# Raw weight chunks through three buffers, then five, then seven

## The chip, the cores and the metric

The kernel runs on one core of a Trainium2 chip. The metric is the device time of one execution in microseconds (us). Five engines work side by side, each through its own queue in order: TensorE (PE in the profile; its weight loads are PEld), VectorE (DVE), ScalarE (ACT), GpSimd (POOL) and SyncE (SP). SP computes nothing here and issues most of the DMAs; POOL issues most of the others.

## The reference, cut to what matters

A two-layer generator works on 256 context tokens and 256 latent tokens, 1024 wide, in fp32. Layer 0 mixes tokens with a bidirectional mLSTM, layer 1 with latent attention (MLA) over context and latent tokens. A gated convolutional FFN (2816 wide) follows each mixer. Around each sub-layer stands a modulation by a condition vector and a post-layer normalisation:

```python
ml = _modulation(c, ada_w[i], ada_b[i])
hl = _modulate(x, ml[0], ml[1])
...
x = _layer_norm(ALPHA * x + ml[2] * yl, ln_g[i, 0], ln_b[i, 0])
f = _conv_ffn(_modulate(x, ml[3], ml[4]), ffn_w_in[i], ffn_conv_w[i], ffn_conv_b[i], ffn_w_out[i])
x = _layer_norm(ALPHA * x + ml[5] * f, ln_g[i, 1], ln_b[i, 1])
```

The context stream needs layer 0 whole, and of layer 1 only its keys and values. The output is the latent stream.

## The kernel before

**Products.** Each fp32 operand is split in two: a high part, rounded to the matmul's type, and a low part, the rest. A product then takes three matmuls (`mm3`, lines 311 to 315): high by high, high by low, low by high.

**Weights.** All weights but the modulations' lie in the array `ws` as chunks of 128 x 1024 fp32 (512 KB; a few are narrower), in the order in which they are used. `_plan` writes that order down: up, og, v, gates, qk, mout (mLSTM), fin0, fout0 (first FFN, with the three dkv chunks of attention ahead of the last six of fout0), ukn, uv, dq, uqr, uqn, aout (attention), fin1, fout1 (second FFN). `Stream` takes each chunk through three steps. `_load` (line 236) lets SP issue a DMA into a raw buffer (tag "raw", three of them). `_split` (line 244) casts the high part on ScalarE (line 257) and subtracts it on VectorE for the low part (line 258); from then on the raw buffer is free. After that `_split` loads further, until three chunks (`NRAW`) beyond the split ones are on their way. `use` hands the parts to the matmuls.

**Two kinds of split buffers.** A narrow chunk goes into one of three pairs (tag "w", the profile's tile w). A wide one, marked in `_plan`, takes two of the 31 general tiles (tag "u", tile wu), so that the last chunks of a stage and the first of the next can be ready at once: `TAIL` says how many chunks at a stage's end are multiplied row tile by row tile, `WIDE` how many are split into general tiles. The general tiles also hold activations, probabilities and normalised rows. `pump` and `st.limit` say how far splits may go at a boundary.

**Boundaries.** After mout, fout0, aout and fout1 stands a normalisation (`ln_rows`, lines 943 to 987): VectorE multiplies by the gate (953), adds the residual (954), takes statistics (956, 958); ScalarE takes the root (960), VectorE the reciprocal (961) and the negative mean (963), and both write the normalised rows (984, 985, 982). `ln_T` (1003) transposes them on TensorE (1011), applies the modulation (1018, 1020) and splits the result (1023, 1024). The context's dkv rows go through `rms` (1140 to 1143) and `dkv_T` (1191).

**Other users of the tags.** Modulations after the start are made on VectorE in the background: `ada_bg` (line 428) loads 128 x 1024 blocks of `ada_w` into two tiles of tag "ar" and sums into two tiles of tag "acc". The order on SP shows the last of these done during fin0. `rope_load` (line 1238) puts the rotary table into the two "ar" tiles; its last reader is `rope_rows`, for the queries, before attention's heads. The start-up also uses both tags, once.

**Order.** The order of instructions on each engine outside the start-up is set by a scheduler that goes by priorities and by when it takes operands and buffers to be ready. So a buffer that is free earlier can also change the order of other work in the queues of PE, DVE, ACT and SP.

Of the kernel before, what the change touches and what calls it, by code (L numbers as in the profile page):

```python
# [7 lines left out]
F32 = mybir.dt.float32  # L8
# [21 lines left out]
CW = 1024  # L30

NB, NRAW, NU = 3, 3, 31
# [189 lines left out]
class Stream:  # L222


    def __init__(self, k, ids, order, ws):
# [4 lines left out]
        self.limit = self.n  # L230
        self.raw, self.hl = {}, {}

    def skip(self, n):
        self.nl = self.ns = self.nu = n

    def _load(self):
        k, j = self.k, self.nl
        n, cols = self.ids[self.order[j][0]]
        t = k.pool.tile([128, CW], F32, tag="raw", name="raw", bufs=NRAW)
        k.nc.sync.dma_start(t[:, :cols], self.ws[n, :, :cols])  # L240
        self.raw[j] = t
        self.nl += 1

    def _split(self):
        k, j = self.k, self.ns
        key, wide = self.order[j]
        cols = self.ids[key][1]
        while self.nl <= j:
            self._load()
        raw = self.raw.pop(j)  # L250
        if wide:
            h, l = [k.pool.tile([128, CW], F32R, tag="u", name="wu", bufs=NU) for _ in range(2)]
        else:
            w = k.pool.tile([128, 2, CW], F32R, tag="w", name="w", bufs=NB)
            h, l = w[:, 0], w[:, 1]
            self.live.append(j)
        k.nc.scalar.copy(h[:, :cols], raw[:, :cols])  # L257
        k.nc.vector.tensor_sub(l[:, :cols], raw[:, :cols], h[:, :cols])  # L258
        self.hl[j] = (h, l)
        self.ns += 1  # L260
        while self.nl < min(self.ns + NRAW, self.n):
            self._load()

    def use(self, key, hold=False):
# [1326 lines left out]
```

## Time and profile before

| | us |
|---|---|
| median of three runs (lowest, highest) | 1431.02 (1429.1, 1434.94) |
| the profiled execution | 1429.89 |
| its span, first to last instruction | 1428.1 |
| TensorE busy | 1398.6 |
| VectorE busy | 980.5 |
| ScalarE busy | 642.3 |
| mean granted TensorE clock (share of full) | 0.996 |

The page's groups give the price of one instruction: a cast of a chunk on ScalarE (L257) 1.05 us, a subtraction on VectorE (L258) 1.21 us, a raw load 3.9 us from issue to landing (median of 300). Matmuls are pipelined: one of 512 columns is listed with 0.39 us, but the timeline shows them 0.23 us apart. A line "A <- B: total, times, longest" among the waits says how long engine A stood idle until B released it. In the timeline the columns are start, duration, engine, line, operation, tiles and count, with the idle time before it and its releaser in brackets. In the stretches, the columns are the length, then busy time and count by engine, the clock, the DMA engines' busy share and GB/s.

### The profile page before, as it was taken

Reading aid. Unit: us, or ns where it says so; the run is one execution under the profiler, and the core shown is the slowest. Engines: PE = TensorE matmul, PEld = TensorE weight load, DVE = VectorE, ACT = ScalarE, POOL = GpSimd, SP = SyncE. Lnnn points to the kernel's source line nnn. Section 1 sums busy time; section 2 is a strip of 40 time slices with the busy share of each in tenths; the row PEclk is TensorE's granted clock in tenths of the full one; section 3 lists DMA queues with packets and bytes.
Section 4 is the critical chain, followed back from the end, with each engine's and each line's share of the span. In section 5 each row is a group of like instructions: output and inputs, shape, how many; then the busy total and the mean of one; then the engine's idle time right before and its main releaser. Section 6 shows DMA issues by size and latency. Waiting matters only on the chain.

```text
span 1428.1 us, 18819 instructions
## 1 busy us (share of the span) xinstructions
PE 1398.6 (98%) x7095; PEld 1176.5 (82%) x7095; DVE 980.5 (69%) x1437; ACT 642.3 (45%) x972; POOL 100.1 (7%) x185
## 2 busy tenths in 40 slices
PE   7999999999999999999999999999999999899997
PEld 3788888888888888888888888888887998899986
DVE  6696778885775666666787444444567888777755
ACT  6554231224334254464553333334364665555542
POOL 0010110003001010210001000000000001000000
PEclk9999999999999999999999999999999999999999
DMA  9475776777774745555635333335666315367763
GB/s 335 172 240 185 238 250 220 253 232 269 252 230 154 221 136 173 178 178 179 207 129 193 91 116 116 121 123 171 191 187 208 122 53 183 124 187 216 223 198 102
DMA packets 82827, 262.70 MB, mean 184 GB/s; under 512 B 11352, under 2 KB 19752, under 8 KB 82736
## 3 DMA queue, kind: packets, MB, share of 16 engines
q1 hardware_dynamic: 68304, 214.82, 48.2%
q0 software_dynamic: 14144, 46.17, 9.6%
q8 instruction: 55, 0.90, 0.3%
q10 hardware_dynamic: 288, 0.52, 0.1%
q14 instruction: 36, 0.29, 0.1%
HBM read 243.56 MB, written 17.91 MB: 183 GB/s over the span
## 4 chain that ended last, share of the span: by engine, by line
PE 65%; issue 18%; DMA 6%; DVE 6%; ACT 3%; POOL 2%; SPq 0%; DVEq 0%; POOLq 0%; ACTq 0%
PE fin L315 8%; PE fin L313 8%; PE fin L314 8%; PE y L314 5%; PE y L315 5%; PE y L313 5%; PE qk L315 4%; PE qk L313 4%; PE qk L314 4%; DMA raw<-in_ws 3%; DMA ar<-in_ada_w 2%; DVE wu L258 1%; PE up L313 1%; DMA xcr<-xcd 1%; PE up L315 1%
## 5 line engine op out<-in xcount | busy, mean ns | idle before, releaser
L258 DVE TENSOR_TENSOR w<-raw,w 128x1024 fp32r<-128x1024 f32 (+2 forms) x267 | 323.9, 1213 | 240.2 <-ACT w L257 239.7
L257 ACT CAST w<-raw 128x1024 fp32r<-128x1024 f32 (+2 forms) x267 | 278.6, 1045 | 437.2 <-PE tok L315 153.3
L315 PE MATMUL fin<-h,w 128*128 128x256 f32 (+1 forms) x696 | 231.6, 333 | 0.5 <-DVE w L258 0.5
L314 PE MATMUL fin<-h,w 128*128 128x256 f32 (+1 forms) x696 | 231.8, 333 | 0.0
L313 PE MATMUL fin<-h,w 128*128 128x256 f32 (+1 forms) x696 | 231.7, 334 | 0.0
L440 DVE SCALAR_TENSOR_TENSOR acc<-ar,cond,acc 128x1024 f32<-128x1024 f32 x112 | 140.6, 1279 | 36.0 <-DMA ar<-in_ada_w 35.6
L315 PEld LDWEIGHTS fin<-h,w 128*128 128x128 f32 x696 | 132.2, 190 | 13.8 <-DVE w L258 0.9
L314 PEld LDWEIGHTS fin<-h,w 128*128 128x128 f32 x696 | 132.2, 190 | 13.0 <-DVE h L1024 0.2
L313 PEld LDWEIGHTS fin<-h,w 128*128 128x128 f32 x696 | 132.0, 190 | 12.8
L313 PE MATMUL qk<-xc,w 128*128 128x512 f32 x256 | 101.1, 395 | 0.0
L313 PE MATMUL tok<-w,xm 128*128 128x512 f32 x256 | 100.4, 392 | 0.0
L315 PE MATMUL qk<-xc,w 128*128 128x512 f32 x256 | 100.1, 391 | 0.2 <-DVE w L258 0.2
L314 PE MATMUL qk<-xc,w 128*128 128x512 f32 x256 | 99.9, 390 | 0.0
L315 PE MATMUL tok<-w,xm 128*128 128x512 f32 x256 | 99.7, 389 | 0.0
L314 PE MATMUL tok<-w,xm 128*128 128x512 f32 x256 | 99.6, 389 | 0.0
L313 PE MATMUL y<-w,act 128*128 128x512 f32 (+1 forms) x212 | 80.4, 379 | 0.0
L315 PE MATMUL y<-w,act 128*128 128x512 f32 (+1 forms) x212 | 80.1, 378 | 0.0
L314 PE MATMUL y<-w,act 128*128 128x512 f32 (+1 forms) x212 | 80.1, 378 | 0.0
L258 DVE TENSOR_TENSOR wu<-raw,wu 128x1024 fp32r<-128x1024 f32 x36 | 43.9, 1222 | 21.7 <-ACT wu L257 21.3
L315 PEld LDWEIGHTS qk<-xc,w 128*128 128x128 f32 x256 | 48.1, 188 | 10.6 <-DVE w L258 0.6
L313 PEld LDWEIGHTS tok<-w,xm 128*128 128x128 f32 x256 | 48.0, 188 | 10.3
L315 PEld LDWEIGHTS tok<-w,xm 128*128 128x128 f32 x256 | 48.1, 188 | 10.1
(357 smaller groups left out, 2756.6 us busy)
## 6 DMA issues: line engine op xcount, KB each, us to landing
raw<-in_ws SPq DMA_DIRECT2D x300, 512.0 KB, 3.9
ar<-in_ada_w SPq DMA_DIRECT2D x80, 512.0 KB, 4.5
adaw<-in_ada_w SPq DMA_DIRECT2D x32, 256.0 KB, 6.5
xcd<-cv POOLq DMA_DIRECT2D x16, 256.0 KB, 3.2
od<-o POOLq DMA_DIRECT2D x16, 256.0 KB, 4.0
vd<-v POOLq DMA_DIRECT2D x16, 256.0 KB, 3.9
xcr<-xcd POOLq DMA_DIRECT2D x16, 256.0 KB, 6.7
vr<-vd POOLq DMA_DIRECT2D x16, 256.0 KB, 3.8
```

The source lines that it names most:

```text
L257: k.nc.scalar.copy(h[:, :cols], raw[:, :cols])
L258: k.nc.vector.tensor_sub(l[:, :cols], raw[:, :cols], h[:, :cols])
L313: mm(out, w[0], x[0], start=start, stop=False)
L314: mm(out, w[0], x[1], start=False, stop=False)
L315: mm(out, w[1], x[0], start=False, stop=stop)
L440: nc.vector.scalar_tensor_tensor(acc[j], w, s, acc[j], op0=ALU.mult, op1=ALU.add)
```

## The change

From the first chunk of fout0 on, raw chunks go round five tiles: three of tag "raw" and the two of tag "acc". From the first chunk of aout on they go round seven: these five and the two of tag "ar". The number of chunks loaded beyond the split ones follows: three, five, seven. `ring` gives the list of tiles that holds for a chunk; the load's DMA, the casts and all the matmuls stay as they are.

```diff
+        keys = [x[0] for x in order]
+        self.bufs = [(0, [("raw", NRAW)] * NRAW)]
+        self.bufs.append((keys.index(("fout0", 0, 0)), self.bufs[-1][1] + [("acc", 2)] * 2))
+        self.bufs.append((keys.index(("aout", 0, 0)), self.bufs[-1][1] + [("ar", 2)] * 2))
+
+    def ring(self, j):
+        return [x for x in self.bufs if x[0] <= j][-1]
...
-        t = k.pool.tile([128, CW], F32, tag="raw", name="raw", bufs=NRAW)
+        j0, ring = self.ring(j)
+        tag, bufs = ring[(j - j0) % len(ring)]
+        t = k.pool.tile([128, CW], F32, tag=tag, name="raw", bufs=bufs)
...
-        while self.nl < min(self.ns + NRAW, self.n):
+        while self.nl < min(self.ns + len(self.ring(self.ns)[1]), self.n):
```

No tile is added, and none gets larger: the tags exist before with the same sizes.

## The prediction

> **What bounds the kernel now.** The page's busy line comes first: TensorE is busy for 1398.6 of 1428.1 us. So a change that moves no matmul can win only what TensorE stands idle, some 30 us, and what a slower clock costs it.
>
> ```profile
> PE 1398.6 (98%) x7095; PEld 1176.5 (82%) x7095; DVE 980.5 (69%) x1437; ACT 642.3 (45%) x972; POOL 100.1 (7%) x185
> ```
>
> Next, where it stands idle: the busy time in stretches of 10 us. In the first 30 us it stands idle for 9.9 us (start-up), and from 1420 us to the end for 8 us (the last normalisation). Neither has a weight chunk in it that the change could bring earlier. From fout0's start at about 975 us, where the change begins, to 1410 us, the idle time sums to 9.7 us: 1.8 at 1080 to 1110 us, 1.1 at 1130 to 1200 us, 0.7 at 1200 to 1210 us, 5.4 at 1220 to 1230 us, 0.8 at 1400 to 1410 us. That, and the clock, is all there is.
>
> Then the waits around the boundary from attention's output projection to the second FFN (1195 to 1232 us), by total:
>
> ```profile
> ACT wu L257 <- DMA raw<-in_ws: 6.1, 4, 3.2
> PEld zT L1011 <- DVE z L984: 5.2, 1, 5.2
> PE zT L1011 <- DVE z L984: 5.0, 1, 5.0
> DVE wu L258 <- ACT wu L257: 3.1, 3, 2.8
> ACT w L257 <- DMA raw<-in_ws: 2.5, 1, 2.5
> ```
>
> TensorE waits 5.0 us for the normalised rows (L984). Behind that, ScalarE waits 8.6 us in five waits for raw chunks, and VectorE 3.1 us for ScalarE's casts. ScalarE's timeline there shows what stands behind these waits in its queue:
>
> ```profile
> 1201.97 1.05 ACT L257 CAST wu<-raw 128x1024 fp32r<-128x1024 f32 x1
> 1206.27 1.05 ACT L257 CAST wu<-raw 128x1024 fp32r<-128x1024 f32 x1 [3.25 <-DMA raw<-in_ws]
> ...
> 1212.28 1.06 ACT L257 CAST wu<-raw 128x1024 fp32r<-128x1024 f32 x1 [2.28 <-DMA raw<-in_ws]
> 1215.82 1.05 ACT L257 CAST w<-raw 128x1024 fp32r<-128x1024 f32 x1 [2.48 <-DMA raw<-in_ws]
> 1216.78 1.04 ACT L257 CAST wu<-raw 128x1024 fp32r<-128x1024 f32 x1
> 1217.84 1.28 ACT L960 ACT_TABLE_LOAD   x1
> ```
>
> The splits come late, among the normalisation's own work. That loads wait for buffers, not for the transfer engines, is seen in the stretch 1160 to 1175 us: nothing moves there, as all three buffers are full.
>
> ```profile
> core 0: us, PE busy (x) PEld busy (x) DVE busy (x) ACT busy (x) POOL busy (x), PEclk, DMA share, GB/s
> 1160.00:1175.00 15.00, 15.00 (x104) 13.69 (x103) 12.26 (x27) 9.90 (x23) 0.55 (x1) 1.00 0.00 0
> ...
> 1224.50:1232.00 7.50, 4.66 (x23) 4.67 (x24) 5.45 (x14) 4.80 (x12) 0.00 (x0) 0.54 0.47 142
> ```
>
> The second row is the other cost: after the gap, the granted clock is 0.54 over 1224.5 to 1232 us, and 1.00 on both sides. Last, the chain of waits at the end of fout1, which is the cycle of one buffer: land, cast, subtract, load again.
>
> ```profile
> 1384.95 1.23 DVE wu L258
> 1386.20 4.45 DMA raw<-in_ws
> 1390.67 1.06 ACT wu L257
> 1391.75 1.24 DVE wu L258
> 1393.00 4.62 DMA raw<-in_ws
> ```
>
> **The change, part by part.** Nothing is added or removed: on each engine the changed program has as many instructions of each kind, the same DMAs and the same bytes. What moves is when a raw chunk's DMA may issue, and with it the order in each queue. One cycle takes 4.5 + 1.06 + 1.24 = 6.8 us, so three buffers bring at most a chunk each 2.3 us; five allow 1.4 us and seven 1.0 us, so that VectorE's 1.2 us a split is the next limit.
>
> *975 to 1070 us and 1232 to 1380 us: 0.* TensorE is at 10.00 of 10 us in nearly every stretch here; the splits wait for split buffers that TensorE frees ("ACT w L257 <- PE y L315"). If that cover were gone, the page's lines for fin, y and tok name a weight wait of 0.5 us at most.
>
> *End of fout0, five buffers: -0.7 us.* From 1075 to 1110 us ScalarE waits 10.8 us in eight waits for raw chunks; TensorE loses 0.45 us to a split at 1085.2 us and about 0.3 us to context rows and transposes that stand behind these casts. In the changed order two of the six wide splits go ahead of the last dkv chunk, and the other four directly behind it; all stand before the context rows' square sums. So the 0.7 us goes. The 1.04 us at 1106.7 us (zT waits for L984) I leave standing: VectorE is nearly full from 1090 to 1107 us, and the four splits of ukn and uv still stand among the normalisation's steps. Bounds: 0 to 1.7 us.
>
> *Attention to FFN, seven buffers: -3.5 us.* With seven, the chunk seven ahead loads as soon as one is split, and the first three chunks of fin1 land during attention. Of the next four, the first loads when the fifth aout chunk is split (1201.9 us) and the others 1.2 us apart; with the 4.2 us median landing here, they are there by about 1206 to 1210 us, or 1211 us at this stage's 235 GB/s (2.1 MB). ScalarE's casts in the changed order: nine of 1.0 us from 1202 us, one wait of 1 to 2 us for a chunk, the last done at about 1213 us, not 1222.8. VectorE, walked in the changed order with the durations of before: four splits to 1208 us; the first row half's product at about 1208.5 us; then five splits (5 x 1.13) between twelve steps of 0.6 us and the short ones, with the first rows' mean at 1215.6 us. The last product of y needs TensorE's end at 1220.3 us (1220.94 less the 0.69 us wait at 1207.4 us, which goes); from there 0.4 + 0.3 + 0.4 + 0.2 us to the mean and, as before, 1.5 us over the root to the transposes: 1223.4 us in place of 1227.34. That is 3.9 us. For the wait at 1207.4 us nothing is added, since it lies in that chain. I take 3.5, because some splits may still slip between the last steps at 1.2 us each; bounds 1.5 and 4.5.
>
> *End of fout1: -0.8 us.* The chain above ends in a TensorE wait of 0.77 us at 1406.7 us. With seven buffers the changed order casts wide chunks alternately with the narrow ones, from the fourth-last narrow one on, so these are ready long before. What is late next is TensorE itself (12 matmuls 0.227 us apart, 2.7 us a chunk, against 1.2 us of VectorE). Bounds 0 and 0.8.
>
> *Issues on SP.* One raw load moves ahead of a small write of a modulation (gd); SP then holds that write for at most one buffer's cycle, 6.8 us, and its reader comes many microseconds later: 0. The loads that now share the engines with POOL's transfers: the gates (5.1 us to land, issued 1183.8 us) and residuals (3.5 us, from 1174.3 us) are first read at 1211 us, so a landing twice as long is still hidden: 0.
>
> *The clock: 0, between a gain of 2.0 and a loss of 2.0 us.* At the slow clock 12 transposes took 2.5 us (0.21 each; at 1.00 they stand about 0.13 apart) and 2 us of fin ran at half pace: 2.0 us lost in all. Shorter idle time may spare it; or it begins at the same moment and covers more matmuls. [...]
>
> **Sum.** 0.7 + 3.5 + 0.8 = 5.0 us. The profiled execution took 1429.9 us (span 1428.1 and 1.8 around it): 1424.9 us after. The runs shown have their median 1.1 us above it, at 1431.0 us, so I predict **1426.0 us**, 0.35% less.
>
> **Rivals.** A measurement of this kernel can tell about 0.5% (7.2 us) from no change; faster by that means under 1423.9 us, slower over 1438.2.
> - *The gap gets short enough that the clock stays up.* For it: TensorE's own idle time (transposes counted as work) falls from 5.0 us to about 2. [...] It saves 2.0 us, and if also the 1.04 us at 1106.7 us goes, 3.0: 1431.0 - 8.0 = 1423.0 us. Chance 0.26.
> - *Hidden anyway:* the splits come earlier, but VectorE (12.7 of 15 us busy at 1220 to 1235 us) is the bound of each boundary, and only the two weight waits go (0.45 + 0.77): 1429.8 us. Chance 0.14.
> - *Slower: the root waits in ScalarE's queue.* In the changed order all nine casts stand ahead of the first L960, before it seven of them. The root is wanted at about 1215.6 us, with casts done at 1213: 2.6 us of slack. If the four last chunks land more than 2.6 us later than worked out, each further microsecond delays every later row. At half the rate (118 GB/s) they end at 1219.7 us, the chain about 6 us later than forecast, and with 2 us of fin at half clock more: 1426.0 + 6 + 2 = 1434 us. If the half clock lasts another 7 us (3.5 us lost) or the same happens at fout0's end, 1438 to 1441. Chance 0.12, of which 0.07 beyond 1438.2.
>
> The forecast keeps 0.48. Range: 1421.0 (all gains at their upper bounds and half of the runs' scatter) to 1433.0 us. Faster by over 0.5%: the first rival nearly whole and the forecast's edge, 0.28; slower: 0.07 and 0.02 for a wait that I haven't seen, 0.09; within: 0.63.
>
> **What would show it.** Right: ScalarE's waits for raw at 1195 to 1232 us fall from 8.6 to under 3 us, the zT wait from 5.0 to about 1.5 to 2.5, the waits at 1085 and 1406 us are gone, TensorE's busy time is unchanged. Wrong: waits for raw stay or move behind L960; the 0.54 stretch is longer; or a new wait of fin for w, or of y for wu, is in the list.

## The result, and the profile after

The changed kernel takes 1423.93 us (median of six runs, 1423.38 to 1425.17); the kernel before, run beside it, 1430.68 us (six runs, 1429.1 to 1434.94). The medians are 6.75 us apart. The ratio is 0.9947, with a 95% interval of 0.9937 to 0.9957. The profiled execution took 1423.38 us, with a span of 1421.6 us and a mean granted clock of 0.997. Lines of the changed part stand 10 lower in the new kernel's file: the cast L257 is now L267, the subtraction L268, the normalised rows L994, the first FFN matmul L323.

The page's busy line of the changed kernel:

```profile
PE 1395.9 (98%) x7095; PEld 1176.7 (83%) x7095; DVE 980.3 (69%) x1437; ACT 640.8 (45%) x972; POOL 100.5 (7%) x185
```

There are as many instructions as before, but TensorE's busy time fell by 2.7 us. The prediction said that it would stay; why it fell is told at fout0's end below.

The waits of the changed kernel between attention's output projection and the second FFN (1195 to 1232 us):

```profile
ACT rs L970 <- DVE mv L968: 3.9, 2, 2.7
...
PE zT L1021 <- DVE z L994: 2.7, 1, 2.7
ACT w L267 <- DMA raw<-in_ws: 2.2, 2, 1.8
```

ScalarE's waits for raw chunks fell from 8.6 to 2.2 us. Its longest wait is now for VectorE's statistics. TensorE's wait for the normalised rows fell from 5.0 to 2.7 us. ScalarE's timeline of the changed kernel shows the casts out of the way:

```profile
1201.51 3.90 ACT L267 CAST wu<-raw 128x1024 fp32r<-128x1024 f32 x4
1207.23 1.05 ACT L267 CAST w<-raw 128x1024 fp32r<-128x1024 f32 x1 [1.82 <-DMA raw<-in_ws]
...
1211.48 1.04 ACT L267 CAST wu<-raw 128x1024 fp32r<-128x1024 f32 x1
1212.55 1.28 ACT L970 ACT_TABLE_LOAD   x1
1214.96 0.29 ACT L970 ACTIVATE rs<-mv,keps 128x1 f32<-128x1 f32 x1 [1.13 <-DVE mv L968]
```

The last cast ahead of the root ends at 1212.5 us (before: 1217.8 us), and the root then waits 1.13 us for VectorE's mean, not for a cast. Busy time and clock in three stretches of the changed kernel, with the columns of the stretches shown above:

```profile
1217.50:1222.60 5.10, 2.58 (x22) 2.34 (x21) 4.60 (x12) 1.89 (x4) 0.00 (x0) 1.00 0.79 259
1222.60:1226.10 3.50, 3.28 (x15) 3.21 (x16) 1.81 (x5) 2.88 (x8) 0.00 (x0) 0.52 0.08 30
...
1390.00:1400.00 10.00, 10.00 (x54) 8.58 (x53) 0.00 (x0) 0.00 (x0) 0.00 (x0) 1.00 0.01 2
```

The half clock is still there, but only from 1222.6 to 1226.1 us (3.4 us; 6.8 before). In the last row, near fout1's end, VectorE and ScalarE do nothing: every split is done, where before a cycle of one buffer set the pace.

**Where the time came from.** I cut each trace at the first and last starts of the matmuls into dkv (the context's), y, kn, s (the scores) and fin. All numbers are us.

| stretch | before | before again | after | after again |
|---|---|---|---|---|
| start to fout0's first y | 969.6 | 971.3 | 971.6 | 970.7 |
| last dkv matmul to first kn | 19.5 | 19.2 | 17.9 | 18.0 |
| first to last kn | 37.9 | 37.9 | 37.0 | 37.0 |
| last score to aout's last y | 30.2 | 30.2 | 29.2 | 29.2 |
| aout's last y to fin1's last fin | 136.6 | 137.7 | 133.0 | 134.0 |
| last fin to fout1's last y | 62.3 | 62.0 | 61.1 | 61.1 |
| fout1's last y to the end | 8.5 | 8.5 | 8.1 | 8.1 |
| fout0's first y to the end, in all | 458.5 | 459.3 | 449.9 | 451.0 |
| half clock at fin1's start | 6.8 | 10.2 | 3.4 | 3.4 |

The stretches left out differ by less than 0.1 us. From fout0's start on, where the change begins, the gain is 8.3 to 8.6 us by these pairs. In the part ahead of fout0, TensorE, VectorE, ScalarE and GpSimd have the same instructions in the same order in all kernels here; it takes 969.1 to 974.2 us over the thirteen traces. It carries waits that come and go (qk for its weights 0 to 1.9 us, hnT for oh 0 to 2.3 us, the start-up up to 1.4 us). This is why the two first traces differ by 6.5 us in span and not by 8.6: the trace of after lost 2.0 us ahead of the change. What sets this scatter was not settled. In what follows the time from fout0's start, "the part from fout0", is compared beside the medians.

### The profile page after: what moved, and what is told of

The parts are those of the page before. It is cut to its first block, busy times and chain, and to the rows that moved or that the text cites. A ratio compares the mean times of both kernels' runs of the same rounds, so it can differ in the third digit from the quotient of the medians.

```text
span 1421.6 us, 18804 instructions
## 1 busy us (share of the span) xinstructions
PE 1395.9 (98%) x7095; PEld 1176.7 (83%) x7095; DVE 980.3 (69%) x1437; ACT 640.8 (45%) x972; POOL 100.5 (7%) x185
## 4 chain that ended last, share of the span: by engine, by line
PE 68%; issue 18%; DVE 5%; DMA 5%; ACT 2%; POOL 2%; SPq 0%; DVEq 0%; POOLq 0%; ACTq 0%
PE fin L323 8%; PE fin L325 8%; PE fin L324 8%; PE y L324 6%; PE y L325 6%; PE y L323 6%; PE qk L323 4%; PE qk L325 4%; PE qk L324 4%; DMA ar<-in_ada_w 2%; DMA raw<-in_ws 1%; DMA xcr<-xcd 1%; PE up L323 1%; PE up L325 1%; PE up L324 1%
## 5 line engine op out<-in xcount | busy, mean ns | idle before, releaser
L268 DVE TENSOR_TENSOR w<-raw,w 128x1024 fp32r<-128x1024 f32 (+2 forms) x267 | 324.1, 1214 | 232.3 <-ACT w L267 231.8
L267 ACT CAST w<-raw 128x1024 fp32r<-128x1024 f32 (+2 forms) x267 | 278.9, 1045 | 426.4 <-PE tok L325 148.0
L323 PE MATMUL fin<-h,w 128*128 128x256 f32 (+1 forms) x696 | 231.5, 334 | 0.0
L325 PEld LDWEIGHTS fin<-h,w 128*128 128x128 f32 x696 | 132.2, 190 | 13.8 <-DVE w L268 0.9
L324 PEld LDWEIGHTS fin<-h,w 128*128 128x128 f32 x696 | 132.2, 190 | 12.8 <-DVE h L1034 0.2
L323 PEld LDWEIGHTS fin<-h,w 128*128 128x128 f32 x696 | 132.0, 190 | 13.0
L323 PE MATMUL qk<-xc,w 128*128 128x512 f32 x256 | 101.2, 395 | 0.0
L323 PE MATMUL tok<-w,xm 128*128 128x512 f32 x256 | 100.4, 392 | 0.0
L323 PE MATMUL y<-w,act 128*128 128x512 f32 (+1 forms) x212 | 80.4, 379 | 0.0
L325 PEld LDWEIGHTS qk<-xc,w 128*128 128x128 f32 x256 | 48.1, 188 | 12.7 <-DVE w L268 2.6
L323 PEld LDWEIGHTS tok<-w,xm 128*128 128x128 f32 x256 | 48.0, 188 | 10.3
L323 PEld LDWEIGHTS qk<-xc,w 128*128 128x128 f32 x256 | 48.1, 188 | 10.0
```

The source lines that it names most:

```text
L323: mm(out, w[0], x[0], start=start, stop=False)
L324: mm(out, w[0], x[1], start=False, stop=False)
L325: mm(out, w[1], x[0], start=False, stop=stop)
```

## The experiments

**Before and after once more.** Both kernels again, with no edit.

> The kernel before once more, for a second trace of it. Theory (what lies ahead of fout0, the same program in all runs, scatters by some us from run to run, between 969.6 and 974.2 us to the first y of fout0 in the traces so far): fout0's start anywhere in 969 to 974 us, and from there to the end the same as in the first trace, 458.5 us within 0.5. Rival (the first trace's early part is typical of it and the change moved the early part): fout0's start within 0.5 us of 969.6.

A single run: 1432.66 us. Its fout0 starts at 971.3 us, as expected of the scatter. The part from fout0 took 459.3 us, a little more than the expected 458.5 within 0.5, with a half clock of 10.2 us. The stretch of it:

```profile
1225.00:1235.50 10.50, 6.15 (x30) 6.15 (x31) 8.45 (x21) 6.41 (x15) 0.00 (x0) 0.51 0.37 105
```

So the length of the slow clock is a matter of the run as well as of the kernel: 6.8 and 10.2 us with the same program.

> The change itself, in the same call as the version with the filled gap, and a further trace of it. From the runs so far 1423 to 1425 us; from the first y of fout0 to the end 450 us within 0.6, with a half clock of nothing, 3.4 or 6.8 us before fin1, as the moment falls.

1425.18 us (five runs, 1423.5 to 1425.96), ratio 0.9953 (0.9939 to 0.9966); part from fout0 451.0 us. The result repeats, though the part from fout0 is 0.4 us above what was expected; the cause is told below, at the boundary from attention to the FFN.

**Five only.** The seven never come; five last from fout0 to the end.

```diff
-        self.bufs.append((keys.index(("aout", 0, 0)), self.bufs[-1][1] + [("ar", 2)] * 2))
```

> The change with five tiles from fout0 to the end, never seven. Theory (each boundary gains by itself, because its splits no longer wait for their loads): all of the gain at fout0's end stays, by the two traces 2.5 us (1074.9 to 1139.1 us before took 64.2 us, after 61.7); five tiles bring a chunk each 1.4 us, nearly VectorE's 1.2, so most of the 4.5 us at the next boundary and the 1.5 us at the end of fout1 stay as well: 1424.5 to 1426 us. Rival (seven are what counts, five only help fout0's end): 1428 us. Second rival (the time comes from another order of instructions that happens to suit, not from earlier loads): anything from 1422 to 1432, and the gains of the parts don't add up.

1425.02 us (1422.77 to 1427.33), ratio 0.995 (0.9933 to 0.9966); part from fout0 449.8 us, last score to last y 29.2, last y to last fin 132.6. The part from fout0 is as short as with seven, so the two further buffers bring nothing that the traces show (the median's distance from "three ahead" below, 2.0 us, has its counterpart ahead of fout0: 973.4 against 971.3 us): five already get the splits out of the normalisation's way. In this trace the clock stayed at full speed, with a zT wait of 2.5 us.

**Seven from aout, three until then.** The first step is left out.

```diff
-        self.bufs.append((keys.index(("fout0", 0, 0)), self.bufs[-1][1] + [("acc", 2)] * 2))
-        self.bufs.append((keys.index(("aout", 0, 0)), self.bufs[-1][1] + [("ar", 2)] * 2))
+        self.bufs.append((keys.index(("aout", 0, 0)), self.bufs[-1][1] + [("acc", 2)] * 2 + [("ar", 2)] * 2))
```

> Three tiles up to aout, then seven. Theory: the end of fout0 is as before (its 2.5 us are lost), the rest stays: 1426 to 1427 us. First rival (seven are what counts): 1424 to 1425 us, nothing lost. Second rival (order): no sum to be expected.

1427.55 us (ten runs, 1426.11 to 1429.71), ratio 0.9965 (0.9952 to 0.9978), half a microsecond above what was expected. The stretches around kn are those of before (19.1 and 37.9 us), the later ones those of after (29.2, 133.8, 61.1). So the gain falls into parts that add up: what is won at fout0's end needs the buffers at fout0, and the rest does not. The part from fout0 takes 452.8 us, against 449.9 and 451.0 with the change.

**Seven from fin1, three until then.** As the last, with `("fin1", 0, 0)` in place of `("aout", 0, 0)`.

> Three tiles up to the last FFN, then seven; both earlier boundaries load as before. Theory: only the end of fout1 gains, 0.8 us by the wait, up to 1.5 by the traces: 1429 to 1430 us, and the gap before fin1 with its half clock of 6.8 us is back. Rival (order): may lie anywhere.

1427.44 us (nine runs, 1425.52 to 1430.69), ratio 0.9969 (0.9957 to 0.9982). I had expected the boundary to keep its time of before, since loads would still run only three ahead through aout. It did not: the last y comes late (31.6 us after the last score), but from there to the last fin it is 131.8 us, and the part from fout0 takes 452.8 us as in the run above. The waits of this kernel, 1195 to 1232 us:

```profile
ACT wu L266 <- DMA raw<-in_ws: 6.6, 3, 3.9
...
PE zT L1020 <- DVE z L993: 2.4, 1, 2.4
```

ScalarE waits 6.6 us for raw chunks, and yet zT waits only 2.4 us (2.7 in the changed kernel). The total of ScalarE's waits is thus not what the boundary hangs on. My reading fell, and the corrected one is this: the first chunks of fin1 lie in the added tiles, which are free; SP issues a load as soon as its tile is free, whatever the loop's count. (Its trace agrees: by fout0's first y, SP has issued two raw loads more than in the kernel before, 336 DMAs against 334, although only chunks of fin1 and fout1 use added tiles.) To keep the boundary as it was, fin1's first chunks must be kept out of the added tiles.

**Three ahead.** All tiles as in the change, but the loop's bound back at three.

```diff
-        while self.nl < min(self.ns + len(self.ring(self.ns)[1]), self.n):
+        while self.nl < min(self.ns + NRAW, self.n):
```

> The tiles go round five and seven as in the change, but no more than three chunks are loaded beyond the split ones. Theory: what counts is how far loads run ahead, not which tiles they use: no gain, 1430 to 1431.5 us, same as before. Rival (where the tiles lie, or the waits on freed tiles, bring part of it): below 1428 us.

1423.04 us (1422.06 to 1423.58), ratio 0.9935 (0.9917 to 0.9953); part from fout0 450.0 us, ScalarE's longest boundary wait for raw 1.8 us and zT 2.7 us, as with the change. The expectation that the loop's bound carries the gain fell. The number of tiles does: the scheduler places a load when its tile is free. Counted on SP and VectorE through aout, six or seven raw loads are out ahead of the subtracted chunks in this kernel, as in the changed one; in the kernel before it is two or three.

**Seven late.** The test of the corrected reading: three tiles through the boundary, seven only from fin1's ninth chunk.

```diff
+        self.bufs.append((keys.index(("fin1", 4, 0)), self.bufs[-1][1] + [("acc", 2)] * 2 + [("ar", 2)] * 2))
```

> Three tiles up to the ninth chunk of the last FFN, then seven. Unlike the run with seven from its first chunk, no chunk that is split at the boundary before fin1 lies in one of the added tiles. Theory: the tiles are what counts, so the boundary is as in the kernel before (last score to last fin matmul 166.8 us there, 163.4 in the run from fin1 on), with its half clock of 6.8 us; only the end of fout1 gains, 62.3 to 61.0 us from last fin to last y: 1429.5 to 1430.5 us. Rival (a gain at fin1's boundary has another cause than the tiles of its own chunks): 1427 to 1428 us as in that run.

1431.92 us (ten runs, 1429.98 to 1433.42), ratio 0.9997 (0.9986 to 1.0007). The boundary is that of before: 30.3 and 137.0 us, half clock 6.8 us, and these waits (1195 to 1232 us):

```profile
PE zT L1020 <- DVE z L993: 5.0, 1, 5.0
ACT wu L266 <- DMA raw<-in_ws: 4.4, 3, 3.3
ACT w L266 <- DMA raw<-in_ws: 3.2, 1, 3.2
```

Apart from the last normalisation, which scatters, only fout1's end shows a gain, 61.1 us in place of 62.3. With added tiles for fin1's first chunks the boundary gains, and without them it does not; that is shown by this run and the one from fin1 together.

**Three for ukn.** Five tiles for fout0 and dkv only, three from ukn to uqn, seven from aout.

```diff
-        self.bufs.append((keys.index(("aout", 0, 0)), self.bufs[-1][1] + [("ar", 2)] * 2))
+        five = self.bufs[-1][1]
+        self.bufs.append((keys.index(("ukn", 0, 0)), self.bufs[0][1]))
+        self.bufs.append((keys.index(("aout", 0, 0)), five + [("ar", 2)] * 2))
```

> The change, but with three tiles again for the chunks from ukn to uqn (five only for fout0 and dkv, seven from aout on). It parts the 2.5 us that fout0's end and the normalisation behind it gained. Theory: the 1.5 us from the last dkv matmul to the first of kn (19.4 before, 17.9 after) hang on fout0's own six wide chunks and stay; the 1.0 us from the first to the last kn matmul (37.9 before, 37.0 after; the 1.04 us wait for the normalised rows) hangs on the four chunks of ukn and uv, whose casts wait for their loads with three tiles, and is lost again: about 1 us slower than the change. Rival (both come from fout0's splits being out of the way earlier): both stay, same time as the change.

1424.06 us (1421.05 to 1424.54), ratio 0.9939 (0.9925 to 0.9953); 18.0 and 37.0 us around kn, as in the changed kernel. My theory, that the earlier loads of ukn and uv bring the gain there, fell. It is enough that fout0's own last splits are out of the way.

**Filling the gap.** The change, and ten matmuls without use (128x512, into a tile that nothing reads) between aout's last y and the transposes before fin1. They add work and leave nothing out.

```diff
+        of = oT[-1]
...
+        idle = k.ps("idle")
+        for _ in range(10):
+            nc.tensor.matmul(idle, of[:, 0, 0:128], of[:, 0], start=True, stop=True)
```

> The change, with ten extra matmuls (128 x 512, result unused) on TensorE between the last y and the transposes of the normalised rows before fin1, 2.3 us of work in a gap of 2.7. They keep TensorE busy and take no engine that the normalisation needs. Theory (the half clock after the gap costs about 0.5 to 1 us, and hangs on TensorE standing idle): no half clock in the records before fin1, and last y to last fin 132 to 132.5 us in place of 133.0: 0.5 to 1 us faster than the change, 1422.5 to 1423.5 us. Rival (the clock follows from something else, or the extra matmuls delay the transposes): half clock as in the change, or zT later by up to 1 us; 1424 to 1425 us.

1421.36 us (1420.72 to 1425.4), ratio 0.9937 (0.9917 to 0.9957). TensorE's timeline of this kernel:

```profile
1217.77 2.46 PE L1570 MATMUL idle<-oT 128*128 128x512 f32 x10
...
1221.18 1.53 PE L1021 MATMUL zT<-ident,z 128*128 128x128 f32 x12 [0.52 <-DVE z L994]
```

and the same transposes in the changed kernel:

```profile
1222.82 2.82 PE L1021 MATMUL zT<-ident,z 128*128 128x128 f32 x12 [2.74 <-DVE z L994]
```

The twelve transposes take 1.53 instead of 2.82 us, and no half clock follows. Last y to last fin takes 132.2 us, against 133.0 and 134.0 with the change.

> The change with the gap before fin1 filled, timed beside the change on the same chip. Theory (the half clock costs the change about 0.8 us): 0.5 to 1.0 us faster than the change, never a half clock before fin1. Rival (the single look was scatter of the part ahead of fout0): no difference between the two.

1422.10 us (1421.93 to 1423.28), ratio 0.9932 (0.992 to 0.9945). The changed kernel ran on the same chip in the same session ("after again", 1425.18 us): each of the five runs with the fill lies below each of its five. The medians are 3.1 us apart, the parts from fout0 1.5 us (449.5 against 451.0); the other pair of traces is 0.8 us apart (449.1 against 449.9). This version is faster than both kernels, by 0.8 to 1.5 us over the change in the part that the fill can touch. The rest of the medians' distance I can't place.

**Two subtractions on GpSimd.** The change, with the subtractions of fin1's fifth and sixth chunk taken from VectorE, to see whether VectorE is the boundary's next limit.

```diff
+        e = k.nc.gpsimd if key[0] == "fin1" and key[1] == 2 else k.nc.vector
+        e.tensor_sub(l[:, :cols], raw[:, :cols], h[:, :cols])
```

> The change, with the subtractions of two chunks (the fifth and sixth of fin1, split among the steps of the normalisation before it) on GpSimd in place of VectorE. Theory (with the change, the last product of y is what VectorE waits for, so VectorE is no longer what bounds this boundary; it takes it up 0.3 us after TensorE): no gain there, last y to the transposes unchanged at 3.1 us, 0 to +1 us in all, as GpSimd is slower. Rival (VectorE is still the bound): two splits of 1.2 us less ahead of the last steps, up to 2 us faster, 1422 us.

1423.48 us (1422.7 to 1424.91), ratio 0.9944 (0.9929 to 0.9959); last y to last fin 133.8 us. No gain, but the run does not show what a freer VectorE would bring, since VectorE did not get free: its own subtractions became slower, and it took up the last product of y 1.4 us after TensorE's last y (0.4 us in the changed kernel). GpSimd's line in this kernel, and VectorE's:

```profile
1206.86 5.99 POOL L269 TENSOR_TENSOR w<-raw,w 128x1024 fp32r<-128x1024 f32 x2 [23.90 <-ACT w L267]
```

```profile
1207.75 2.83 DVE L269 TENSOR_TENSOR wu<-raw,wu 128x1024 fp32r<-128x1024 f32 x1 [0.52 <-ACT wu L267]
1211.70 2.23 DVE L269 TENSOR_TENSOR wu<-raw,wu 128x1024 fp32r<-128x1024 f32 x1
```

While GpSimd's two run (1206.86 to 1212.85 us), VectorE's subtraction takes 2.83 and 2.23 us instead of 1.22.

## Why the prediction was right and wrong

The direction, the mechanism and the range held: 1423.93 us lies between 1421 and 1433, and the boundaries gain where they were said to. The forecast of 1426.0 us was 2.1 us too high. By the traces the change gains 8.6 us from fout0 on (458.5 to 449.9), where the sum said 5.0. So the sum was off by more than the forecast: the medians are only 6.75 us apart, and in the traced pair 2.0 us were lost ahead of fout0, in work that the change does not touch. That the forecast came within 2.1 us is in part luck.

Of the signs named beforehand, ScalarE's waits for raw (2.2 us) and the split waits of TensorE at fout0's and fout1's end came out as said. TensorE's wait for the normalised rows did not fall to 1.5 to 2.5 us but to 2.7, and 3.4 in the second trace; and TensorE's busy time was not unchanged.

**fout0's end: mis-sized, and the step that failed.** The prediction took 0.7 us, the idle time that the trace lists. Measured are 1.6 us up to the first kn and 0.9 more up to the last. TensorE's timeline of the kernel before shows where the rest was hidden:

```profile
1083.50 0.39 PE L313 MATMUL y<-wu,act 128*128 128x512 f32 x1
1083.78 0.50 PE L314 MATMUL y<-wu,act 128*128 128x512 f32 x1
1084.12 0.40 PE L315 MATMUL y<-wu,act 128*128 128x512 f32 x1
...
1085.21 0.49 PE L314 MATMUL y<-wu,act 128*128 128x512 f32 x1 [0.45 <-DVE wu L258]
```

An undisturbed matmul starts 0.23 us after the last but is listed with 0.39 us. So up to 0.16 us of each stall lies inside what is called busy: from 1083.50 to 1083.78 and on to 1084.12 us the starts are 0.28 and 0.34 us apart, with no idle time listed at all. Between 1082.1 and 1101.4 us the starts lie 2.3 us further apart than 72 matmuls at 0.227 us and six transposes need; listed as idle were 0.74. In the changed kernel the same stretch (1084.15 to 1101.86 us) is 1.6 us shorter; 0.7 us of such loss stays, with a listed wait of 0.44 us for the context's rows at 1087.04 us, which the prediction had counted among what goes. The same holds for "TensorE's busy time unchanged": it fell by 2.7 us, because stalls had been counted in it.

The other part is the zT wait of 1.04 us at 1106.7 us, which the prediction left standing because VectorE was nearly full. It went. VectorE's timeline of the kernel before:

```profile
1101.86 0.67 DVE L953 TENSOR_TENSOR z<-y,gate 128x512 f32<-128x512 f32 x1
1102.45 1.21 DVE L258 TENSOR_TENSOR wu<-raw,wu 128x1024 fp32r<-128x1024 f32 x1
1103.58 0.68 DVE L954 SCALAR_TENSOR_TENSOR z<-xres,z 128x512 f32<-128x512 f32 x1
```

and of the changed kernel:

```profile
1101.05 1.21 DVE L268 TENSOR_TENSOR wu<-raw,wu 128x1024 fp32r<-128x1024 f32 x1
1102.17 0.68 DVE L963 TENSOR_TENSOR z<-y,gate 128x512 f32<-128x512 f32 x1
1102.89 0.69 DVE L964 SCALAR_TENSOR_TENSOR z<-xres,z 128x512 f32<-128x512 f32 x1
```

A split whose cast had come late stood between the product and the residual of the last rows; now it stands ahead of them. The normalised rows come 1.1 us earlier (L984 starts 4.65 us after the first kn, L994 3.54 us after it): VectorE was full, and its order was what cost. That the two parts come from fout0's own splits is shown by "three for ukn", and that they need the buffers at fout0 by "seven from aout".

**Attention to FFN: right.** Predicted 3.5 us (worked out as 3.9), measured 4.0: 1.0 up to the last y, and 3.0 from there to the transposes (1222.82 us against 1227.34, with the last y 1.5 us earlier). The last cast was forecast for 1213 us and ended at 1212.5; the first rows' mean was forecast for 1215.6 and ended at 1214.9. Two figures of the working do not come out: its last steps add up to 1223.1 us, not 1223.4, and the ninth cast of the kernel before ended at 1223.7 us, not 1222.8. What carries the gain is shown by "seven late" and "seven from fin1". That it takes seven is not: five do as well.

VectorE's timelines show where the 3.0 us were. In the kernel before, two splits stand between the last product of y and the last rows' statistics:

```profile
1222.39 0.41 DVE L953 TENSOR_TENSOR z<-y,gate 128x256 f32<-128x256 f32 x1
1222.80 1.23 DVE L258 TENSOR_TENSOR w<-raw,w 128x1024 fp32r<-128x1024 f32 x1
...
1224.28 1.22 DVE L258 TENSOR_TENSOR w<-raw,w 128x1024 fp32r<-128x1024 f32 x1
```

In the changed kernel the last split stands ahead of that product:

```profile
1218.52 1.22 DVE L268 TENSOR_TENSOR w<-raw,w 128x1024 fp32r<-128x1024 f32 x1
...
1219.99 0.41 DVE L963 TENSOR_TENSOR z<-y,gate 128x256 f32<-128x256 f32 x1
```

From the start of the last product to the twelve transposes it is 4.94 us in the three traces with these two splits in between (both of the kernel before and "seven late"), and 2.82 to 2.85 us in the ten without. The rest of the 3.0 us is that VectorE took up the last product 1.3 us after TensorE's last y before, and 0.4 us after it in the changed kernel. The prediction let this product wait for TensorE alone, and kept 0.4 us back for splits that slip between the last steps; one did, ahead of the product.

**fout1's end: a little low.** Predicted 0.8, measured 1.0 and 1.2 us in the two pairs, again more than the idle time listed (0.77).

**The clock: it gained, within its bounds.** Predicted 0 with 2.0 us to either side. Of the 3.5 us won between last y and last fin, 3.0 stand in the earlier transposes. The other 0.5 fits the half clock, 3.4 us long instead of 6.8: fin's matmuls ran at half clock for 1.95 us before (1229.81 to 1231.76 us) and for 0.87 us after (1225.31 to 1226.18 us), with starts 0.21 us apart in place of 0.12. By that nearly half of these times is lost, 0.5 us less than before.

That the clock would cost as much behind the shorter gap was the prediction's estimate, and no run shows it. The half clock lasted 3.4 us in both traces of the changed kernel (zT waits of 2.7 and 3.4 us), and 6.8 and 10.2 us in the two of the kernel before (5.0 us in each). In "five only" and "seven from fin1" (waits of 2.5 and 2.4 us) and in both traces with the fill (0.5 us) there was none: the sixteen transposes took 272 or 273 ns each in the median there, against 421 ns in the changed kernel. In the first trace of each kernel the changes of the granted clock lie whole steps of 3.413 us behind the start of its record: 354, 355 and 411 steps from 14.45 us in the changed kernel, 355, 357 and 413 from 13.20 us in the kernel before. In the step ahead of the half clock TensorE was busy for 0.71 us in the changed kernel (1219.36 to 1222.77 us) and for 0.54 us in the kernel before (1221.52 to 1224.93 us). What makes the clock halve, and for how many steps, is not settled.

**The rivals.** The first (1423.0 us, that the clock stays up and the 1106 us wait goes) came nearest in time. It was half right: the wait went, the half clock was halved and not gone. "Hidden anyway" is excluded by the zT wait, 5.0 to 2.7 us. Whether VectorE is the next limit of the boundary the run with GpSimd could not tell, as it slowed VectorE itself, but the traces of the changed kernel do: VectorE has no idle time in the 10 us ahead of the last product, and takes it up 0.4 us after TensorE's last y in the first trace and 1.3 us in the second. Behind it stands one raw chunk still: ScalarE waits 1.8 us for it in the first trace and 2.7 in the second, VectorE's subtraction of it waits 0.26 and 1.17 us, and the transposes come 0.9 us later. "Slower" did not come: ScalarE stood idle for 1.13 us before the root's operand came.

**The rest** of the distance between 5.0 and 8.6 us is 1.8 at fout0's end, 0.5 at the boundary, 0.5 of clock, 0.4 at fout1's end, and 0.4 in the last normalisation, which is scatter (8.1 to 8.6 us over the thirteen traces, 8.1 in "seven late" and 8.6 in "five only").

## What to carry to other kernels

When stalls are added up on a pipelined engine, as TensorE is in this profile, listed idle time is a lower bound (at fout0's end 0.74 us was listed where 2.3 us were lost); take the spacing of starts against that of an undisturbed stretch. With a scheduler that issues a load when its tile is free, the number of tiles sets how far loads run ahead (six or seven here, against two or three), and what matters is which chunks find a free tile at a boundary: five tiles did here what seven did. When a boundary hangs on a chain of short steps, look for long background work in the queue between them. A gap on TensorE costs its own length, and a slow clock can follow it (here 5.0 us of waiting, then 6.8 or 10.2 us at half clock); a few matmuls without use can be worth their place there (ten of them, 0.8 to 1.5 us).

## What the runs showed of the hardware that was not expected

**Subtractions on GpSimd slowed VectorE's.** Two 128x1024 fp32 subtractions took GpSimd 5.99 us (1206.86 to 1212.85 us), and VectorE's of the same size, begun at 1207.75 and 1211.70 us beside them, took 2.83 and 2.23 us; those begun at 1204.69 and 1214.46 us, ahead of GpSimd's and behind them, took 1.22 and 1.21. The second of the slow ones ends 1.08 us after GpSimd's last. What holds VectorE up was not shown.

**The slow clock came in steps of 3.41 us, and not each time alike.** The same program had 6.8 us of it in one trace and 10.2 in another; a zT wait of 2.5 us ("five only") was followed by none, one of 2.7 us (the changed kernel) by 3.4. In the first trace of each kernel all changes of the granted clock lie whole multiples of 3.413 us apart.
